# Four MLP blocks of 384 tokens beside the decode, a last block of 576, and two visits fewer in each round of the decode

## The chip, the cores and the metric

One core of a Trainium2 chip runs the whole step as one program. The metric is the device time of one execution in microseconds; for the kernel before three executions are known.

## The reference

One layer of a hybrid decoder computes 2048 prompt tokens and 8 sequences of 8 new tokens each, against a paged cache of 8192 past tokens a sequence. In short:

```python
h = rmsnorm(x, norm1_g)
b, c, u, q, k, v = split(h @ w_in)                       # 1024 -> 3*512 + 3*512
y_conv = b * conv3(c * u)
o = rmsnorm(diff_attn(q, k, v), subln_g) * 0.8           # 4 heads, two maps each, ALiBi
x = x + concat(y_conv, o) @ w_out                        # 1024 x 1024
h2 = rmsnorm(x, norm2_g)
x = x + square(relu(h2 @ w_up)) @ w_down                 # 1024 -> 4096 -> 1024
y = rmsnorm(x, final_g)
```

For the prompt `diff_attn` goes over the prompt's own keys; for the new tokens (the decode) over the gathered pages of the cache and the new keys. Everything is float32. Dense products are made from two float32r parts of each operand, three matmuls for a product; the decode's products are plain float32.

## The kernel before

Four stages follow one another on the tensor engine (PE). **The input projection** goes over the tokens in three blocks. **The attention** of the prompt is mixed with the convolution's columns and, at its end, with the output projection of the first 384 tokens. **The MLP blocks**: three `Dense` objects of 384 prompt tokens each (three tiles of 128) run one after the other. **The last block** has the 64 new tokens and the other 896 prompt tokens, in two groups of 448 and 512 columns.

Each block streams all of `w_out`, `w_up` and `w_down` again: 8 + 32 + 32 weight tiles of 512 KB, each of which ACT copies to its high part (`wh`, L226) and DVE subtracts to its low part (`wl`, L228). `run` goes over 16 chunks of two weight tiles: `up` (L199 to L201) streams a group's tokens past 128 columns of `w_up`, so the moving width is the group's width; `down` (L1410 to L1412) streams 512 columns of `w_down` past 128 tokens. Before the last chunk's `down` comes the output projection of the next block (`out_proj`, L1299 to L1301), and in the last chunk's `down` its normalised tokens are transposed (`turn`, L1267). `before_last` issues the loads of the next block's mixed input ahead of that.

**The decode** is a generator that the dense code advances. Each dense product calls `between(us)`, which pops a pending closure or else calls `tick(us)`; this adds the product's nominal time to a counter, and once the counter has reached `gap * gs` it runs the generator to its next `yield cost, gap`. Such a piece of decode work between two dense products is called a visit here. Two sequences run beside the input projection, then the generator pauses for the attention; the other six run beside the MLP blocks (`gs` is `GS[0]` in the first, `GS[2]` in the second part). `hold` stops it from the last tile of an output projection to the first products of the next block.

A round of the decode takes a pair of chunks of four pages. DVE transposes the keys (`kt`, L717); PE makes the score maps c = 0 and 1 (`sps`, L902, 16 records a map); for the sequence before, PE transposes the exponentials (`pps`, L937), ACT copies them out (`ptt`, L940), and PE multiplies them with the values of the two chunks e = 0 and 1 (`o_ps`, L949, 32 records a chunk, four heads side by side in 32-column strips of the array). A round has a visit for each map, one for the transposes and one for each value chunk. Behind each value chunk `gather_v` (L707) issues the four indirect DMAs for the chunk after next into the same buffer; there are two such buffers (`vpg`). A sequence has 8 rounds; its values come one sequence behind its scores, so that the first 8 rounds of a part have no values and its last 8 no scores.

When the decode is done, `switch` gives its memory to the last block, whose loads are then issued at `poll` places of the last 384-token block, and what is left in `before_last`, after `drain` has run what is left of the decode.

## Time and profile before

| | us |
|---|---|
| median of three runs | 3242.1 |
| the three runs | 3237.74, 3242.1, 3257.38 |
| span of the profiled execution | 3153.6 |
| median less span | 88.5 |
| MLP block 1 starts | 1141 |
| output projections of blocks 2, 3 and of the last | 1474, 1934, 2341 |
| decode's second part, first and last visit | 1168, 2221 |

The span goes from the first to the last instruction of the profiled execution. No time of that execution other than its span is known; the median of the runs is 88.5 us longer, which is what lies around the span. [...]

### The profile page before, as it was taken

To read this page: it belongs to the slowest core of one execution; us is meant where nothing else is said; L and a number is where in the kernel's file an instruction comes from. 1 tells how busy PE (TensorE), PEld (TensorE's weight loads), DVE (VectorE), ACT (ScalarE), POOL (GpSimd) and SP (SyncE) were. 2 spreads that over 40 slices of the span, in tenths; PEclk is the share of its full clock that TensorE was granted. 3 is DMA by queue.
4 is the path that set the end of the run, shared out by engine and by line. 5 is a ranking of instruction groups with operands and counts; after the bars stand their busy time and mean duration, and the time that the engine had idled before them with its cause. 6 is when DMAs were issued, how large, how long until landed. Compare 5 with 4: busy or idle time off the path is not lost. (4 is left out here: it accounts for less than half of the span.)

```text
span 3153.6 us, 53285 instructions
## 1 busy us (share of the span) xinstructions
PE 3014.2 (96%) x20902; PEld 2532.3 (80%) x20902; DVE 1824.8 (58%) x3751; ACT 1243.3 (39%) x2705; POOL 891.8 (28%) x1266
## 2 busy tenths in 40 slices
PE   7999998999999989999999999999999999999998
PEld 7988887989997788777677777777887788888886
DVE  5376353268888668766676776663653444444444
ACT  3323323357778643333343333343332332222222
POOL 0013355211122121455466564467002010000002
PEclk9999999999999999999999999999999999999999
DMA  4777876754335457899689899677741112111111
GB/s 149 229 232 247 286 255 200 223 140 113 108 99 146 139 176 242 278 320 334 229 288 360 304 347 328 211 274 263 230 145 41 61 54 67 47 54 47 54 47 64
DMA packets 400821, 585.80 MB, mean 186 GB/s; under 512 B 35413, under 2 KB 299605, under 8 KB 384186
## 3 DMA queue, kind: packets, MB, share of 16 engines
q1 hardware_dynamic: 337418, 301.07, 31.1%
q0 software_dynamic: 61984, 277.91, 24.5%
q8 instruction: 165, 2.70, 0.3%
q10 hardware_dynamic: 1168, 3.41, 0.3%
q14 instruction: 86, 0.70, 0.1%
HBM read 526.56 MB, written 55.74 MB: 185 GB/s over the span
## 5 line engine op out<-in xcount | busy, mean ns | idle before, releaser
L707 POOL DMA_INDIRECT vpg<-in_cache_v_dram,pt x512 | 537.5, 1050 | 232.3 <-issue 134.4
L226 ACT CAST wh<-wraw 128x1024 fp32r<-128x1024 f32 x336 | 350.0, 1048 | 632.2 <-PE dps L1412 277.1
L228 DVE TENSOR_TENSOR wl<-wraw,wh 128x1024 fp32r<-128x1024 f32 x336 | 410.2, 1221 | 236.4 <-ACT wh L226 227.4
L199 PE MATMUL ups<-h2h,wh 128*128 128x384 f32 (+2 forms) x1264 | 462.6, 366 | 4.9 <-DVE x L1417 2.5
L1417 DVE TENSOR_TENSOR x<-dps,x 128x512 f32<-128x512 f32 (+1 forms) x528 | 355.2, 684 | 177.2 <-PE dps L1412 176.7
L1410 PE MATMUL dps<-wh,uh 128*128 128x512 f32 (+1 forms) x1076 | 438.8, 408 | 13.2 <-ACT wh L226 5.6
L201 PE MATMUL ups<-h2h,wl 128*128 128x384 f32 (+2 forms) x1264 | 448.8, 355 | 0.0
L200 PE MATMUL ups<-h2l,wh 128*128 128x384 f32 (+2 forms) x1264 | 447.9, 354 | 0.0
L1411 PE MATMUL dps<-wl,uh 128*128 128x512 f32 (+1 forms) x1076 | 425.5, 395 | 4.3 <-DVE wl L228 3.3
L1412 PE MATMUL dps<-wh,ul 128*128 128x512 f32 (+1 forms) x1076 | 424.2, 394 | 0.0
L199 PE MATMUL ps<-hh,wh 128*128 128x384 f32 (+1 forms) x1152 | 404.6, 351 | 1.1 <-ACT cc L1526 0.7
L201 PE MATMUL ps<-hh,wl 128*128 128x384 f32 (+1 forms) x1152 | 376.5, 327 | 3.1 <-DVE wl L228 3.1
L200 PE MATMUL ps<-hl,wh 128*128 128x384 f32 (+1 forms) x1152 | 376.0, 326 | 0.1
L1369 DVE TENSOR_TENSOR ul<-r,uh 128x384 fp32r<-128x384 f32 (+2 forms) x158 | 93.6, 592 | 438.5 <-ACT uh L1368 438.3
L717 DVE STREAM_TRANSPOSE kt<-kraw 128x512 f32<-128x512 f32 x512 | 316.9, 678 | 5.4 <-DMA kraw<-in_cache_k_dram,idxk 5.4
L699 POOL DMA_INDIRECT kraw<-in_cache_k_dram,idxk x128 | 129.1, 1009 | 565.6 <-DVE kt L717 522.8
L199 PEld LDWEIGHTS ups<-h2h,wh 128*128 128x128 f32 x1264 | 238.5, 189 | 54.4 <-issue 28.7
L1410 PEld LDWEIGHTS dps<-wh,uh 128*128 128x128 f32 (+1 forms) x1076 | 200.8, 187 | 85.8 <-issue 24.1
L1366 ACT ACTIVATE r<-ups 128x384 f32<-128x384 f32 (+2 forms) x158 | 82.8, 524 | 445.0 <-PE ups L201 445.0
L200 PEld LDWEIGHTS ups<-h2l,wh 128*128 128x128 f32 x1264 | 238.9, 189 | 16.6
L201 PEld LDWEIGHTS ups<-h2h,wl 128*128 128x128 f32 x1264 | 238.5, 189 | 15.3
L284 POOL TENSOR_SCALAR ss<-ss 128x1 f32<-128x1 f32 (+1 forms) x33 | 9.5, 289 | 839.5 <-ACT junk L276 838.7
(275 smaller groups left out, 4985.8 us busy)
## 6 DMA issues: line engine op xcount, KB each, us to landing
wraw<-in_w_up_dram SPq DMA_DIRECT2D x128, 512.0 KB, 5.0
wraw<-in_w_down_dram SPq DMA_DIRECT2D x128, 512.0 KB, 3.3
wraw<-in_w_in_dram SPq DMA_DIRECT2D x72, 512.0 KB, 4.4
wraw<-in_w_out_dram SPq DMA_DIRECT2D x32, 512.0 KB, 4.2
x<-in_x_prompt_dram SPq DMA_DIRECT2D x24, 512.0 KB, 7.0
vpg<-in_cache_v_dram,pt POOLq DMA_INDIRECT x512
qt<-QH SPq DMA_DIRECT2D x64, 128.0 KB, 4.5
qt<-QL SPq DMA_DIRECT2D x64, 128.0 KB, 5.0
```

The costliest lines, as they stand in the source:

```text
L199: nc.tensor.matmul(ps, lhsT=wh, rhs=ah, start=first, stop=False)
L200: nc.tensor.matmul(ps, lhsT=wh, rhs=al, start=False, stop=False)
L201: nc.tensor.matmul(ps, lhsT=wl, rhs=ah, start=False, stop=last)
L226: nc.scalar.copy(wh, t)
L228: eng.tensor_sub(wl, t, wh.bitcast(F32))
L699: nc.gpsimd.indirect_dma_start(out=t.rearrange("p a b -> p (a b)"), out_offset=None, in_=ck, in_offset=bass.IndirectOffsetOnAxis(ap=idxk[: ...
L707: nc.gpsimd.indirect_dma_start(out=t[:, g, :], out_offset=None, in_=cv, in_offset=bass.IndirectOffsetOnAxis(ap=idxv[:, 4 * it + g:4 * it + ...
L717: nc.vector.transpose(t[:, e, 16 * j:16 * j + 16].rearrange("p a b -> p (a b)"), kraw[2 * r + e][:, 16 * j:16 * j + 16].rearrange("p a b - ...
L1410: nc.tensor.matmul(ps, lhsT=uh, rhs=wh[:, half], start=(i == 0), stop=False)
L1411: nc.tensor.matmul(ps, lhsT=uh, rhs=wl[:, half], start=False, stop=False)
L1412: nc.tensor.matmul(ps, lhsT=ul, rhs=wh[:, half], start=False, stop=(i == len(ms) - 1))
L1417: nc.vector.tensor_add(xx, ps, xx)
```

## The change

The first three of four changes are in the order of the work; the last is a set of constants.

- `NDS = 4`: four `Dense` blocks of 384 tokens (1536 prompt tokens) run beside the decode; the last block has the new tokens and 512 prompt tokens, in groups of 320 and 256 columns. The weight stream has one more pass.
- The two score maps of a round are one visit (`yield 2.1`), and the two value chunks are one visit (`yield 2.4`); both chunks' gathers are issued behind the merged visit.
- The gap that stood between the maps moves behind the transposes, the one between the chunks to the end of the merged visit.
- `GS` goes from (0.7, 0.7, 0.7) to (0.75, 0.7, 1.15).

With GP2 = (2, 1, 2, 3, 2, 2, 3, 3) the gaps of a full round beside the MLP still add up to 12, now in four visits or pauses where there were six. Lines that only lose comments are left out here.

```diff
-GS = (0.7, 0.7, 0.7)
+GS = (0.75, 0.7, 1.15)
+NDS = 4
...
                     for c in range(2):
                         for db in range(2):
                             for h in range(H):
...
-                        yield 1.05, gp()[0] if c else gp()[1]
+                    yield 2.1, gp()[0]
...
-                    yield 0.4, gp()[3]
+                    yield 0.4, gp()[3] + gp()[1]
                     for e in range(2):
                         it = NCH * pb + 2 * i + e
                         v = vpg.pop(it)
...
-                        if it + 2 < b1 * NCH:
-                            gather_v(it + 2)
+                    for e in range(2):
+                        if NCH * pb + 2 * i + e + 2 < b1 * NCH:
+                            gather_v(NCH * pb + 2 * i + e + 2)
                         more(MO[3 + e])
-                        yield 1.2, gp()[4 + e]
+                    yield 2.4, gp()[4] + gp()[5]
...
-        W = Weights(wpA, out_weights() + mlp_weights(out_weights()) * 3 + mlp_weights([]), 2, 4, SHR)
-        ds = [Dense([ptiles(384 * i, 384 * i + 384)], ac1, xslots(i), EN1 and nc.gpsimd) for i in range(3)]
+        W = Weights(wpA, out_weights() + mlp_weights(out_weights()) * NDS + mlp_weights([]), 2, 4, SHR)
+        ds = [Dense([ptiles(384 * i, 384 * i + 384)], ac1, xslots(i), EN1 and nc.gpsimd) for i in range(NDS)]
...
-        slots = xslots(3) + [(sm, f"x1_{ti}") for ti in range(3, 8)]
-        d = Dense([[(xs, ys, 0, NS)] + ptiles(1152, 1536), ptiles(1536, 2048)], sm, slots, ENG and nc.gpsimd)
+        slots = xslots(NDS) + [(sm, f"x1_{ti}") for ti in range(3, 5)]
+        t0 = 384 * NDS
+        d = Dense([[(xs, ys, 0, NS)] + ptiles(t0, t0 + 256), ptiles(t0 + 256, T)], sm, slots, ENG and nc.gpsimd)
...
-        elif box and box["todo"] and cur[0] == 2:
+        elif box and box["todo"] and cur[0] == NDS - 1:
...
-        if cur[0] < 2:
+        if cur[0] < NDS - 1:
...
-        if i < 2:
+        if i < NDS - 1:
             rest.append(lambda: load_gain("2", nc.gpsimd))
-        if i == 0:
-            rest += [lambda ti=ti: ds[2].load_x(ti, nc.gpsimd) for ti in range(3)]
+        if i < NDS - 2:
+            rest += [lambda i=i, ti=ti: ds[i + 2].load_x(ti, nc.gpsimd) for ti in range(3)]
```

## Rows read from the trace of the kernel before

**Rows 1.** The page of the profiled execution, its parts 1 and 2: busy time of the tensor engine (PE) with its share of the span, and the busy tenths of GpSimd (POOL, which issues the gathers of the decode) in 40 slices of 78.8 us.

```profile
PE 3014.2 (96%) x20902; PEld 2532.3 (80%) x20902; DVE 1824.8 (58%) x3751; ACT 1243.3 (39%) x2705; POOL 891.8 (28%) x1266
...
POOL 0013355211122121455466564467002010000002
```

**Rows 2.** Busy time by stage: the stretch, its length, then busy us and number of instructions of PE, PEld (weight loads), DVE, ACT and POOL, the granted clock of PE, the DMA share and GB/s. In order: input projection with the decode's first two sequences; MLP block 1; from the output projection of block 2 to that of block 3; block 3 while the decode still runs; the rest of block 3; the last block behind its output projection.

```profile
112.00:612.00 500.00, 478.08 (x4136) 428.64 (x4135) 238.56 (x483) 162.43 (x348) 171.82 (x186) 0.99 0.74 239
1141.00:1474.00 333.00, 324.88 (x2528) 258.22 (x2529) 247.83 (x441) 124.69 (x225) 127.84 (x122) 0.99 0.84 288
1474.00:1934.00 460.00, 437.29 (x3940) 333.58 (x3939) 313.79 (x579) 167.07 (x333) 269.02 (x289) 0.99 0.87 309
1934.00:2221.00 287.00, 266.20 (x2305) 208.18 (x2303) 162.55 (x281) 108.43 (x216) 159.62 (x185) 0.96 0.74 253
2221.00:2341.00 120.00, 116.56 (x580) 105.36 (x581) 72.28 (x100) 48.73 (x71) 0.00 (x0) 0.99 0.68 219
2437.00:3154.00 717.00, 700.34 (x3140) 577.57 (x3138) 308.92 (x436) 193.72 (x290) 45.76 (x106) 0.99 0.18 56
```

**Rows 3.** The timeline of PE around one visit to the score maps (L902) between products of the output projection: start, length, instruction, count.

```profile
1515.87 0.39 PE L1301 MATMUL ps<-wh,mxl 128*128 128x512 f32 x1
1516.19 1.07 PE L902 MATMUL sps<-kt,qbd 128*32 128x256 f32 x16
1517.19 0.50 PE L1299 MATMUL ps<-wh,mxh 128*128 128x512 f32 x1
1517.53 0.40 PE L1300 MATMUL ps<-wl,mxh 128*128 128x512 f32 x1
```

**Rows 4.** The same around a visit to one chunk of cached values (L949, 32 records) and, in the second half, around the visit to the new tokens' values at the end of a sequence (L975, 8 records of the same kind).

```profile
1502.78 0.39 PE L1301 MATMUL ps<-wh,mxl 128*128 128x512 f32 x1
1503.10 1.07 PE L949 MATMUL o_ps<-vpg,ptt 128*16 128x128 f32 x32
1504.10 0.50 PE L1299 MATMUL ps<-wh,mxh 128*128 128x512 f32 x1
1504.43 0.40 PE L1300 MATMUL ps<-wl,mxh 128*128 128x512 f32 x1
...
1631.11 0.40 PE L1412 MATMUL dps<-wh,ul 128*128 128x512 f32 x1
1631.43 0.41 PE L975 MATMUL o_ps<-vn_s,pttn 64*16 64x128 f32 x8
1631.77 0.50 PE L1410 MATMUL dps<-wh,uh 128*128 128x512 f32 x1
1632.11 0.40 PE L1411 MATMUL dps<-wl,uh 128*128 128x512 f32 x1
```

**Rows 5.** The timeline of PE for narrow products: in the input projection the change from 384 to 320 columns, each product with a weight tile of its own; in the attention six score products of 256 columns, and what starts behind them.

```profile
200.78 0.34 PE L201 MATMUL ps<-hh,wl 128*128 128x384 f32 x1
200.96 0.30 PE L199 MATMUL ps<-hh,wh 128*128 128x320 f32 x1
201.10 0.31 PE L200 MATMUL ps<-hl,wh 128*128 128x320 f32 x1
201.25 0.31 PE L201 MATMUL ps<-hh,wl 128*128 128x320 f32 x1
...
750.81 0.98 PE L1832 MATMUL asc<-kst,qt 128*128 128x256 f32 x6
751.63 0.38 PE L1908 MATMUL aT<-ident,S 128*128 128x128 f32 x2
```

**Rows 6.** Waits of PE at the change from block 1 to block 2, 1474 to 1541 us: who waited for whom, us in total, times, longest.

```profile
PE ps L1299 <- ACT wh L226: 3.2, 1, 3.2
PE ps L1300 <- DVE wl L228: 2.7, 3, 1.2
PE tps L1267 <- DVE x L1417: 1.6, 1, 1.6
PE tps L1267 <- DVE h2l L1270: 1.6, 1, 1.6
```

**Rows 7.** The same at the change from block 2 to block 3, 1934 to 2002 us, the waits that rows 6 don't have.

```profile
PE o_ps L949 <- ACT ptt L940: 4.1, 1, 4.1
...
PE dps L1410 <- ACT wh L226: 1.0, 1, 1.0
PE dps L1411 <- DVE ss L286: 0.8, 1, 0.8
```

**Rows 8.** The two longest waits of PE while the decode runs beside the MLP, 1141 to 2241 us.

```profile
PE o_ps L949 <- DMA vpg<-in_cache_v_dram,pt: 14.4, 18, 1.9
PE o_ps L949 <- ACT ptt L940: 10.0, 4, 5.0
```

**Rows 9.** The same for the decode's first two sequences, 112 to 612 us.

```profile
PE o_ps L949 <- DMA vpg<-in_cache_v_dram,pt: 6.2, 7, 2.3
PE o_ps L949 <- ACT ptt L940: 3.3, 2, 1.7
```

**Rows 10.** The timeline around one late page: two of the eight value gathers of a pair of chunks on POOL (the second of them, and the last of the second chunk), then the last piece of the first chunk's value products on PE, which begins when its page lands (in brackets the idle time before it).

```profile
1674.71 0.95 POOL L707 DMA_INDIRECT vpg<-in_cache_v_dram,pt  x1 [0.30 <-issue]
...
1683.28 0.94 POOL L707 DMA_INDIRECT vpg<-in_cache_v_dram,pt  x1 [0.30 <-issue]
...
1686.77 0.41 PE L949 MATMUL o_ps<-vpg,ptt 128*16 128x128 f32 x8 [0.86 <-DMA vpg<-in_cache_v_dram,pt]
```

More of the change, by code (lines that the diff above doesn't have):

```diff
@@ L2080, in switch @@
                        for gi in range(2) for g in range(2) for x in "hl"]
-        box["todo"] += [lambda ti=ti: d.load_x(ti) for ti in list(range(3, 8)) + list(range(3))]
+        box["todo"] += [lambda ti=ti: d.load_x(ti) for ti in list(range(3, 5)) + list(range(3))]
     def poll():
@@ L2103, in tile_hymba_step @@
         cur[0] = i
-        d.run([(sb1, "uh", "ul", 4, 384)], poll, before_last, lambda: ds[cur[0] + 1] if cur[0] < 2 else box["d"], None)
+        d.run([(sb1, "uh", "ul", 4, 384)], poll, before_last, lambda: ds[cur[0] + 1] if cur[0] < NDS - 1 else box["d"], None)
         rest += [lambda: load_gain("f", nc.gpsimd)] + FN * [lambda: None]
```

## The prediction

> **What bounds the kernel now.** I read the page first, then busy time by stage, then the timeline of the tensor engine around the places that the change touches, and last its waits. PE is busy for 96% of the span [rows 1], so only what PE does, or waits for, can move the end. Its lengths overlap; what a product costs is the distance from one start to the next, and the sums below are made of such distances. By stage [rows 2] the kernel is uneven: from 1141 to 2221 us, where six of the eight sequences run beside the MLP, the DMA share is 0.74 to 0.87, and in the 717 us of the last block it is 0.18. GpSimd's digits tell the same [rows 1]: gathers stand in slices 4 to 8 and 17 to 29, and the last ten slices have almost none. The change spreads the decode over more dense work, at the price of one more pass over the weights, and makes three visits of five.
>
> **Fewer visits.** Without a visit a product of 512 columns takes 0.23 us: 717 us over 3140 in the last block [rows 2]; 1517.53 less 1517.19 is 0.34 because the first one behind a visit is late [rows 3]. From the last product before the score visit (1515.87) to the second one behind it (1517.53) are 1.66 us; less two distances of 0.23 that is 1.20 us for the visit. For the values [rows 4] it is 1504.43 less 1502.78, 1.65 less 0.46, or 1.19 us for 32 records; and the small visit, 8 records of the same kind, takes 1632.11 less 1631.11, 1.00 less 0.46, or 0.54. So 24 records more cost 0.65 us, 8 cost 0.22, and 0.32 us of a visit belong to no record: they are paid at the change from full-array products to column strips and back. The score visit shows the same pieces [rows 3]: 0.09 us before it, about 0.13 behind its last group, 0.11 at the product after. Two merges in each of 64 rounds (8 sequences of 8) save 128 times 0.32, **41 us**: 31 beside the MLP, 10 in the input projection. Bounds: only the two pieces that are read directly (0.09 and 0.11), 26 us; if the small visit's records cost nothing of their own, all of its 0.54, 69 us. I take 41, the value that both kinds of visit give. It lies on the path, since PE has no slack.
>
> **The same products in other widths.** `down` and the output projection always stream 512 columns for each tile, and there are 17 tiles before and after: no change. `up` streams the group's width, and the groups 448 and 512 become 384, 320 and 256, each 768 products. The distance is 0.18 to 0.175 at 384 columns and 0.147 at 320 [rows 5], 0.00044 us a column and some 0.006 to 0.012 that no column explains. Three groups instead of two pay that piece 768 times more: **+4 to +9, taken as +5 us**. For 256 columns six starts to the next product take 0.82 us, at most 0.137 each [rows 5], against 0.12 by the slope; the row as it stands would make it +13.
>
> The extra pass over the weights is 72 tiles of 512 KB, with their casts on ACT and subtractions on DVE. Block for block this is work of the kind that the stage already holds, with DVE busy for 314 and ACT for 167 of 460 us [rows 2]. From 1141 to 2341 the four stretches give 337 MB in 1200 us, 281 GB/s [rows 2]. With 38 MB and one block of about 290 us more it becomes 375 MB in some 1480 us, 253 GB/s: the stage where PE waits for pages and weights gets lighter by a tenth, and I cost the pass itself at nothing. Without that cover a tile late by 1 us each time would cost 72 us.
>
> **One more change of blocks.** At a change PE waits for the output weights, which queue on SP behind the next block's mixed input, and for the norms and transposes. The four waits of the first change add up to 9.1 us [rows 6]; the second has 1.8 us beside the 4.1 of the decode's own [rows 7], and the two waits of 1.6 for the transposes again, 5.0 in all. The granted clock falls to its lower level around such waits (0.96 as the mean from 1934 to 2221 us [rows 2], so 23 us at half speed, 11 lost); I count 2 to 4 us of that for a change. The third change that the decode now sees costs 7 to 13 us: **+10**. The change to the last block keeps its form; with 3 and 2 tiles in its groups instead of 4 and 4, fewer products cover the norms: **+3**, 0 to 6.
>
> **The transposed exponentials.** PE waits 10.0 us beside the MLP and 3.3 before for ACT's copy `ptt` [rows 8, 9], in six places, the longest 5.0 and 4.1. Between transposes and values stood 3 gaps times 0.7, 2.1 us of dense work; now it is 4 times 1.15, 4.6, and 5 times 0.75, 3.75 in the first part. Each wait shrinks by 1.6 to 2.5 us and the short ones go: **-9 us**, and with the two long ones some of the lower clock, **-3**. ACT is in order: a copy that stands behind two weight casts can be late all the same, so the bounds are 0 and -16.
>
> **The pages.** PE waits 14.4 and 6.2 us for them [rows 8, 9]. The reason is seen at one late page: gathers follow each other on POOL at 1.43 us (8.57 for six), eight take 11 us, and a piece came 3.5 us behind the last issue of its pair while its own issue lay further back [rows 10]. Behind a merged visit all eight gathers are issued together, from about 1.5 us on; the last page is there after 1.5 + 11 + 4, about 16.5 us. A full round took 12 x 0.7 = 8.4 us of gaps, some 2 for rounding each up to the next product, and 5.2 of visits, about 16; it will take 13.8 + 1.5 + 4.6, about 20. That leaves 3.5 us, as much as the second chunk had before. In the first part, with 13 x 0.75, a round has only 16, and its rounds without scores about 11, but pending closures stretch most of these. What is queued behind a waiting visit on PE is dense work, so a late page is paid in full. One more block's gains, results and tokens also pass POOL's queue ahead of gathers. I take **0**, with -10 (a lighter DMA) and +15 (the first part's short rounds, that queue) as bounds.
>
> **Does the decode end in time?** In dense microseconds its second part needs 37 to begin, 8 rounds without values of about 17.6, 40 full ones of 15.3, 8 without scores of 12.7, and 12 at each of six sequence ends: about 970, and before, by the same reckoning, 650. The trace needed about 720 (1080 us from 1141 to 2221, less 48 rounds of 5.2, some 80 of waits and lower clock, and two stretches of 14 under `hold`), so I raise 970 by a tenth to 1070. A block of 384 has 720 products of 512 columns at 0.23 and 768 of 384 at 0.174, 299 us; the first has 258 left behind the attention. Four offer 3 x 299 + 258, less three stretches of 14: 1113. It ends some 40 to 80 us before the last block's output projection. `drain` finds nothing, but the last block's loads have less time than the 120 us of before [rows 2].
>
> **The sum.** -41 + 5 + 10 + 3 - 9 - 3 + 0 = -35 us. The profiled span is 3153.6 us, so the new one is about 3119; its own time outside the span isn't given, and I carry over the 88.5 us by which the median of the three runs, 3242.1, exceeds it: **3207 us**, 1.1% less. The three runs lie 20 us apart, so a change within 1% (32 us) can hardly be told from none.
>
> **Rivals.** *What is saved at the visits is mostly given back, chance 0.33.* The extra change costs 13 us, 256 columns cost 0.137 us a product (+13), the copies stay late: -41 + 13 + 13 + 3 - 3 = -15, 3227 us. For it: every piece except the merges is small and uncertain. Against: the copy's gap doubles.
>
> *The lower rate clears the waits, 0.17.* Most of the 34 us of waits for pages and copies [rows 8, 9] go, with half of the lower clock (-5), and the rest as forecast: -41 + 5 + 10 + 3 - 30 - 5 = -58, 3184. For it: 281 to 253 GB/s, longer rounds; against: the wait for a page is set by GpSimd's issue, not by bytes [rows 10].
>
> *Merged value visits wait for the second chunk, 0.05: slower.* Place: the second half of each merged visit. It decides once the last of eight gathers lands later than a round, 20 us beside the MLP; 3.5 are left [rows 10], so another 4 us on POOL (a key gather of 1 us that waits for DVE, norms) use it up. If each of the 56 rounds beside the MLP waited 2 us more, +112, less the other gains of 35: +77, 3319. Against: such waits came in 18 of 96 visits and were 0.8 us on average [rows 8]; a wait also gives POOL time to catch up.
>
> *Narrow products are bound by their weight loads, 0.03: slower.* In the last block a load has a length of 0.184 us (577.57 over 3138) [rows 2]. If it hid behind nothing, 256 and 320 columns would take at least 0.184: 768 x (0.064 + 0.037), +78, 3285 us. Against it stands 0.147 at 320 columns, each with its own weights [rows 5]. [...]
>
> *The change doesn't do what it says, 0.02*: the decode isn't done when block 4 ends, and `drain` runs the rest bare, with its chain of copies exposed; 5 rounds at 5 us more, +25 on the forecast, 3232.
>
> **How the numbers follow.** The forecast itself, 3195 to 3218, has 0.40. The range that leaves out 2 in 10 is **3176 to 3241**: it takes in the second rival, the first with its bounds, and the decode's late end, not the two slower ones. Faster by over 1% (below 3209.7) takes 0.23 of the forecast's chance, all of the second rival's 0.17 and 0.10 of the first's that lie at its better bounds: 0.50. Slower by over 1% (above 3274.5) is the two slower rivals, less what a milder form gives: 0.07. The rest is 0.43.
>
> **What the new profile would show.** Right: 64 score visits of 32 records and 64 value visits of 64, each about 2.05 us by starts; three changes of blocks with 5 to 9 us of waits; `ptt` below 5 us in the waits; the DMA share around 0.75 beside the decode; `up` at 256 columns 0.12 to 0.137 us apart; last decode visit 40 to 80 us before the last output projection. Wrong: page waits above 30 us, a change of blocks above 15, or narrow products at 0.18.

## The result, and the profile after

The changed kernel took 3296.1 us (median of four runs), the kernel before 3249.7 in runs beside it: ratio 1.0140, 95% interval 1.0099 to 1.0182. The forecast was 3207 us, 1.1% less; the time is 1.4% more. The profiled execution of after has a span of 3301.5 us and a time of 3303.3: 1.8 us lie around the span, not 88.5 as the table ahead of the prediction has it.

That difference is the first finding, and the rest can't be read without it. The runs of this study came from different chips, and the same kernel before took 3254.7 and 3275.0 us on two of them and 3156.1, 3157.0 and 3154.9 on three others. The trace shown ahead of the prediction (span 3153.6) agrees with the three; the three times shown beside it (3242.1) and the result above agree, by their length, with the two. In what follows a chip of the **first kind** is one where before takes 3240 us or more, one of the **second kind** one where it takes about 3155. Each chip was seen on one occasion only, so that what is called a kind of chip may as well be a state that it was in. A ratio is always to before on the same chip.

From the page of after: busy time of PE, the digits of GpSimd and of PE's granted clock in 40 slices, and the queue that brings instructions.

```profile
PE 3060.2 (93%) x21670; PEld 2638.1 (80%) x21670; DVE 1910.0 (58%) x3861; ACT 1332.0 (40%) x2873; POOL 889.1 (27%) x1274
...
POOL 1022244201221121224454333544334520110001
PEclk9998998999999999999999999999999999999999
...
q8 instruction: 171, 2.80, 0.3%
```

PE's share of the span falls from 96% [rows 1] to 93%, and GpSimd's gathers now reach over four blocks. By stage (length, then busy time and instructions of PE, PEld, DVE, ACT and POOL, granted clock, DMA share, GB/s): the input projection behind the first 112 us, the four blocks, the last one.

```profile
112.00:706.00 594.00, 535.89 (x4334) 484.26 (x4332) 246.73 (x494) 169.47 (x364) 166.33 (x186) 0.94 0.65 211
1098.00:1511.00 413.00, 389.27 (x2456) 331.51 (x2455) 279.63 (x512) 180.77 (x355) 85.19 (x127) 0.97 0.60 199
1511.00:1957.00 446.00, 406.74 (x3201) 326.19 (x3201) 272.80 (x476) 157.16 (x293) 189.63 (x218) 0.97 0.74 253
1957.00:2397.00 440.00, 403.02 (x3202) 327.77 (x3201) 271.18 (x472) 156.41 (x291) 192.10 (x217) 0.97 0.74 253
2397.00:2786.00 389.00, 360.94 (x2578) 306.89 (x2577) 215.96 (x339) 151.56 (x265) 131.43 (x155) 0.97 0.64 211
2786.00:3301.50 515.50, 497.17 (x2815) 429.20 (x2813) 250.52 (x363) 172.98 (x302) 39.06 (x100) 0.99 0.25 82
```

Against [rows 2] two things changed: the granted clock (0.94 in the input projection, where before had 0.99, and 0.97 in all four blocks) and PE's busy share of the blocks (0.91 to 0.94, where before had 0.93 to 0.98). In the whole trace PE stood at the lower of its two levels (0.50, against 1.00) for 210 us, in before for 88. At the lower one a product of 384 columns takes 0.32 us from start to start (475.22 to 475.54), at the upper one 0.18 (479.34 to 479.52); with half of it counted as lost, the 121 us more are worth 61. The input projection is 62 us longer than in the trace of before (594 against 532, both from 112 us to the first score product of the attention), though no block was added there.

What PE waited for, after: first in the input projection (112 to 706 us), then from the first output projection to the last (1098 to 2786 us); in us, times, longest.

```profile
...
PE sps L903 <- issue: 9.3, 18, 1.0
...
PE o_ps L950 <- DMA vpg<-in_cache_v_dram,pt: 3.3, 3, 1.9
```

```profile
PE dps L1413 <- DVE wl L229: 29.5, 21, 5.1
PE ups L200 <- DVE x L1419: 13.8, 7, 5.1
PE sps L903 <- issue: 13.7, 23, 1.0
PE dps L1412 <- ACT wh L227: 11.0, 5, 4.6
PE ps L1302 <- DVE wl L229: 7.7, 6, 3.0
```

The waits of [rows 8] and [rows 9] have all but gone: pages 3.3 us, copies 3.0 in both stretches together (1.9 of them `ptt`, the rest the copy for the new tokens). Two others stand in their place. Weights that are cast and subtracted too late (all lines of the second view that name `wh` or `wl` give 54.9 us; 12.4 in the trace of before), and "issue" at the score visits, time in which the engine waited for nothing that the trace shows.

By their median the visits are what the sum took them for. The timeline of PE in after, around a score visit, a value visit, and in the last block's `up` at 256 columns:

```profile
1289.98 0.40 PE L1414 MATMUL dps<-wh,ul 128*128 128x512 f32 x1
1290.31 1.93 PE L903 MATMUL sps<-kt,qbd 128*32 128x256 f32 x32
1292.17 0.50 PE L1412 MATMUL dps<-wh,uh 128*128 128x512 f32 x1
1292.51 0.40 PE L1413 MATMUL dps<-wl,uh 128*128 128x512 f32 x1
...
1706.42 0.39 PE L1414 MATMUL dps<-wh,ul 128*128 128x512 f32 x1
1706.74 1.94 PE L950 MATMUL o_ps<-vpg,ptt 128*16 128x128 f32 x64
1708.61 0.50 PE L1412 MATMUL dps<-wh,uh 128*128 128x512 f32 x1
1708.94 0.40 PE L1413 MATMUL dps<-wl,uh 128*128 128x512 f32 x1
...
3015.37 0.28 PE L200 MATMUL ups<-h2h,wh 128*128 128x256 f32 x1
3015.49 0.28 PE L201 MATMUL ups<-h2l,wh 128*128 128x256 f32 x1
```

By starts less two distances of 0.23, as in [rows 3] and [rows 4]: 2.53 less 0.46 is 2.07 us for the scores, 2.52 less 0.46 is 2.06 for the values. The median over all 64 of each kind, from the last product ahead to the first behind, is 2.18 and 2.19; the means are 3.10 and 2.41. The distance at 256 columns is 0.119 us, the median of 753.

A score visit in the input projection shows where the mean of the scores comes from:

```profile
466.57 0.33 PE L202 MATMUL ps<-hh,wl 128*128 128x384 f32 x1
466.84 1.06 PE L903 MATMUL sps<-kt,qbd 128*32 128x256 f32 x14
468.14 0.64 PE L903 MATMUL sps<-kt,qbd 128*32 128x256 f32 x5 [0.24 <-issue]
469.57 0.63 PE L903 MATMUL sps<-kt,qbd 128*32 128x256 f32 x4 [0.79 <-issue]
470.99 1.10 PE L903 MATMUL sps<-kt,qbd 128*32 128x256 f32 x5 [0.80 <-issue]
472.45 1.03 PE L903 MATMUL sps<-kt,qbd 128*32 128x256 f32 x3 [0.36 <-issue]
473.87 0.61 PE L903 MATMUL sps<-kt,qbd 128*32 128x256 f32 x1 [0.39 <-issue]
474.42 0.69 PE L200 MATMUL ps<-hh,wh 128*128 128x384 f32 x1
```

The first 14 records start at once; the others come up to five at a time, the groups 1.43 us apart, and the visit takes 7.9 us in place of 2.2. None of these instructions has a wait. Call such places **gaps**: 0.6 to 1.3 us from one start to the next before an instruction without a wait, counted from 112 us on, less 0.23 each. After has 56 of them, 35.6 us in all.

### The profile page after: what moved, and what is told of

The parts are those of the page before. It is cut to its first block, busy times and chain, and to the rows that moved or that the text cites. A ratio compares the mean times of both kernels' runs of the same rounds, so it can differ in the third digit from the quotient of the medians.

```text
span 3301.5 us, 55431 instructions
## 1 busy us (share of the span) xinstructions
PE 3060.2 (93%) x21670; PEld 2638.1 (80%) x21670; DVE 1910.0 (58%) x3861; ACT 1332.0 (40%) x2873; POOL 889.1 (27%) x1274
## 4 chain that ended last, share of the span: by engine, by line
PE 58%; issue 14%; POOL 9%; DVE 8%; DMA 5%; ACT 4%; another core or an unknown queue 2%; SPq 0%; ACTq 0%; POOLq 0%; DVEq 0%
POOL vpg L708 6%; PE ups L200 5%; PE ups L202 5%; PE dps L1413 5%; PE dps L1414 5%; PE dps L1412 5%; PE ups L201 5%; PE ps L200 4%; PE ps L202 4%; PE ps L201 4%; PE asc L1834 3%; PE O L1921 3%; PE sps L903 2%; DVE kt L718 2%; PE o_ps L950 2%
## 5 line engine op out<-in xcount | busy, mean ns | idle before, releaser
L227 ACT CAST wh<-wraw 128x1024 fp32r<-128x1024 f32 x408 | 425.6, 1048 | 681.2 <-PE dps L1414 168.5
L229 DVE TENSOR_TENSOR wl<-wraw,wh 128x1024 fp32r<-128x1024 f32 x408 | 500.4, 1227 | 318.7 <-ACT wh L227 273.5
L708 POOL DMA_INDIRECT vpg<-in_cache_v_dram,pt x512 | 528.9, 1033 | 357.8 <-PE o_ps L950 215.2
L200 PE MATMUL ups<-h2h,wh 128*128 128x384 f32 (+2 forms) x1520 | 501.0, 330 | 17.6 <-DVE x L1419 13.8
L202 PE MATMUL ups<-h2h,wl 128*128 128x384 f32 (+2 forms) x1520 | 494.2, 325 | 5.7 <-DVE wl L229 4.1
L201 PE MATMUL ups<-h2l,wh 128*128 128x384 f32 (+2 forms) x1520 | 492.0, 324 | 0.7 <-issue 0.7
L200 PEld LDWEIGHTS ups<-h2h,wh 128*128 128x128 f32 x1520 | 288.1, 190 | 39.3 <-issue 27.0
L202 PEld LDWEIGHTS ups<-h2h,wl 128*128 128x128 f32 x1520 | 288.0, 189 | 9.1 <-DVE wl L229 6.1
L201 PEld LDWEIGHTS ups<-h2l,wh 128*128 128x128 f32 x1520 | 288.5, 190 | 4.2 <-issue 1.7
L1413 PEld LDWEIGHTS dps<-wl,uh 128*128 128x128 f32 (+1 forms) x1076 | 203.6, 189 | 84.8 <-DVE wl L229 44.2
```

Source lines behind the costliest of these rows:

```text
L200: nc.tensor.matmul(ps, lhsT=wh, rhs=ah, start=first, stop=False)
L201: nc.tensor.matmul(ps, lhsT=wh, rhs=al, start=False, stop=False)
L202: nc.tensor.matmul(ps, lhsT=wl, rhs=ah, start=False, stop=last)
L227: nc.scalar.copy(wh, t)
L229: eng.tensor_sub(wl, t, wh.bitcast(F32))
L708: nc.gpsimd.indirect_dma_start(out=t[:, g, :], out_offset=None, in_=cv, in_offset=bass.IndirectOffsetOnAxis(ap=idxv[:, 4 * it + g:4 * it + ...
```

## The experiments

Four theories. *Occasion*: the trace of before is of an execution that does not stand for its times. *Supply*: at certain places of the program PE gets its instructions late, and a visit of many records that falls there is drawn out. *Pages*: merged value visits wait for the second chunk (the third rival of the prediction). *Pace*: the wider gap of 1.15 beside the MLP has a price of its own. Two of these are called otherwise in the first expectations: instruction theory stands for supply, and pass theory there says that the extra pass over the weights costs the time.

### Both kernels and each half of the change, on a chip of the first kind (before 3254.7)

**Before, unchanged.** 

> The kernel before, unchanged, so that its profile comes from the same chip as the others'. Occasion theory: the profiled execution that the forecast used (span 3153.6 us) was some 85 us faster than its timed runs, and what lies around a span is 2 us, as in the profile of the changed kernel (3303.31 against 3301.5); then this profile has a span of 3235 to 3262 us and its PE waits for 'issue' inside the score visits and for late weight parts (over 30 us together), as the changed kernel's. Change theory: the profile is like the first (span about 3155, no such waits), and those waits are the change's own.

Ratio 1.0007 (0.9976 to 1.0037), span 3244.8 us: the base is 91 us above the trace of before, as the occasion theory had it, and 1.8 lie around the span. There are 46 gaps of 28.0 us; the trace of before has none. Two lines of its waits that the earlier trace doesn't have:

```profile
PE sps L902 <- issue: 13.2, 21, 1.0
...
PE o_ps L949 <- issue: 9.8, 17, 1.6
```

**The merges alone** (three blocks, gaps of 0.7).

```
-                        yield 1.05, gp()[0] if c else gp()[1]
+                    yield 2.1, gp()[0]
...
-                    yield 0.4, gp()[3]
+                    yield 0.4, gp()[3] + gp()[1]
...
-                        yield 1.2, gp()[4 + e]
+                    yield 2.4, gp()[4] + gp()[5]
```

> The merged visits alone, with three blocks of 384 and the old pace. Instruction theory (a visit of 32 score matmuls in a row outruns the supply of PE's instructions): the 41 us of saved switches are taken back by 'issue' waits inside the score visits, 64 visits at 0.9 us, 58 us, so +10 to +25 us on the kernel before. Pass theory (the extra pass and change of blocks cost the time): -25 to -45 us.

3327.7 us, ratio 1.0243 (1.0198 to 1.0289). That is some 75 us more than before, far over the 10 to 25 of the instruction theory, and against the pass theory. 65 gaps of 38.0 us, 41 waits for pages of 40.3 us, 249 us at the lower clock against 129. The input projection behind 112 us takes 593 us, 549 in before on this chip.

**The blocks alone** (four of 384 and one of 576, gap of 1.15, five visits; against before).

```
-GS = (0.7, 0.7, 0.7)
+GS = (0.7, 0.7, 1.15)
+NDS = 4
```

> Four blocks of 384 and the slower pace beside the MLP (GS 0.7, 0.7, 1.15), with the old five visits a round. Pass theory: +40 to +80 us on the kernel before, and the changed kernel is faster than this one by 25 to 45. Instruction theory: +10 to +25 us (the one more change of blocks), with few 'issue' waits.

3225.1 us, ratio 0.9926 (0.9903 to 0.9948): faster than both kernels on this chip, where both theories had expected it slower. 9 gaps of 4.9 us, 134 us at the lower clock, but 47.8 us of waits for weights beside the MLP.

**After, again.** 

> The changed kernel again, beside the three others on one chip: +35 to +60 us on the kernel before by all theories. If the occasion theory holds, the sum of its waits exceeds that of the profile of the kernel before taken here by no more than 60 us, not by 150.

3284.6 us, ratio 1.0125 (1.0075 to 1.0174). So here blocks and pace give 24 us and the merges take 65 (1.0125 less 0.9926 of 3254.7); by the medians it is 30 and 59. With the merges the gap of the first part went from 0.7 to 0.75, so the 65 are of both. 40 of them stand in the input projection, where two of the eight sequences run: 586 us behind 112 us, 546 with the blocks alone. 45 gaps of 29.4 us, where the same program without merges has 4.9. The gaps are not scattered: of the 64 score visits, numbers 10, 14 and 16 took 9.7, 7.6 and 7.8 us in the trace of after and 8.7, 7.8 and 8.2 here, and none of the first nine met a gap in either. Of the 17 visits in each trace that took over 1 us more than the median, 13 are the same, one of them late only through a wait for its keys. Most belong to places of the program.

### Halves and pace, on a chip of the second kind (before 3156.1)

**Score maps merged, values not** (blocks and gap as in the run with the blocks alone). 

> The four blocks and gaps of 0.7, 0.7, 1.15 as in the run with the blocks alone (3225.1 us), and of the merges only that of the two score maps; the value chunks stay two visits. The supply theory: at certain places of the program PE goes on with four records every 1.43 us although no instruction waits for anything (23.6 us of such gaps inside score visits after the change, 2.2 with the blocks alone), a visit of 32 score records that falls on such a place is drawn out, and the lower clock follows. It expects 3255 to 3285 us, 15 us or more of such gaps in score visits, and over 170 us at the lower clock. The page theory: the merges lose through the value visits, which wait for the second chunk. It expects 3205 to 3225 here.

3197.6 us, ratio 1.0126 (1.0088 to 1.0164), and no gap at all in the trace, in this run or in any other of this kind of chip. As a ratio the supply theory's range was 1.000 to 1.009 and the page theory's 0.985 to 0.991. It is above both, and what PE waits for beside the MLP are weights, 54.5 us.

**Values merged, score maps not.** 

> The other half: blocks and gaps as in the run with the blocks alone, value chunks in one visit, the two score maps in two. The supply theory expects 3205 to 3230 us (64 changes of mode at 0.32 us saved, some pages later) and fewer than 8 us of gaps in score visits. The page theory expects 3255 or more, with over 30 us of waits for pages.

3197.3 us, ratio 1.0148 (1.0105 to 1.0190). No gap; pages 15.9 us, half of what the page theory wanted, and weights 65.1 beside the MLP. What both runs share with each other, and not with before, are the four blocks and the pace.

**Four blocks at the old pace**, five visits (the line of the pace, against after).

```
-GS = (0.75, 0.7, 1.15)
+GS = (0.7, 0.7, 0.7)
```

> Four blocks of 384 and a last one of 576, five visits as before the change, and all gaps 0.7 as before. It tells the extra block from the pace. If the gain of the blocks alone (3225.1 against 3254) comes from the wider gap of 1.15 beside the MLP, this is at or over the kernel before: 3254 plus 5 to 15 for the third change of blocks and the narrower groups, 3255 to 3270, and the decode ends before the fourth block is half done. If the gain comes from the blocks (a shorter last block, more dense work), it is 3220 to 3235.

3168.5 us, ratio 1.0045 (1.0024 to 1.0066): the extra block costs 14 us (8 to 21), as the first case of the expectation had it. PE's waits:

```profile
PE o_ps L950 <- DMA vpg<-in_cache_v_dram,pt: 21.6, 26, 2.4
...
PE o_ps L950 <- ACT ptt L941: 13.6, 10, 4.5
...
PE dps L1411 <- ACT wh L227: 5.4, 3, 2.5
...
PE dps L1412 <- DVE wl L229: 4.4, 8, 1.0
```

Pages and copies as in the kernel before, and hardly any wait for weights, although the extra pass over them is there.

**Half of the score products left out.** 

> The changed kernel with half of the score products left out (one of the two halves of the inner dimension), so that the merged visit has 16 records, as many as a split one had; all visits, gaps, transfers and copies stay. By the medians of the visits (2.18 us with 32 records, 1.30 with 16) the missing work is worth 64 times 0.88, 56 us. The supply theory expects that the gaps inside score visits go too (below 5 us, from 23.5) and a good part of the extra lower clock (45 us at half speed against the blocks alone): 3284.6 less 56, 19 and some 15 is about 3195, at most 3210. If the loss has another place (value visits, the gathers issued together, the longer rounds), only the 56 go: 3228, with the lower clock at 175 us or more.

3147.3 us, ratio 0.9974 (0.9957 to 0.9992). On a chip without gaps it can't tell the supply theory. Against after on this kind of chip (next) it gave 24 us for 56 of missing work: PE waits more for weights (66.5 us beside the MLP, 56.7 in after) and stands longer at the lower clock (164 against 151).

### After, and the pace without and with merges, on a second chip of that kind (before 3157.0)

**After, once more.** 

> The changed kernel once more, because the first four runs and the next four came from different chips: the kernel before took 3254.7 us on the one and 3156.1 on the other, where no trace shows a gap of 0.6 to 1.3 us without a wait. If this chip is of the second kind: the pace theory (the gap of 1.15 makes weight subtractions late on DVE, 50 to 65 us of waits in the MLP in all four runs that have it, 13.6 where the gap is 0.7) expects a ratio to before of 1.010 to 1.020, with 50 us or more of waits for weights beside the MLP; the supply theory alone expects 0.985 to 1.0, since without those gaps the forecast should come true. If it is of the first kind, 1.0125 again.

3173.2 us, ratio 1.0051 (1.0035 to 1.0067). No gap. The visit shown above, the sixteenth to the scores, takes 2.13 us here:

```profile
427.43 0.33 PE L202 MATMUL ps<-hh,wl 128*128 128x384 f32 x1
427.69 1.93 PE L903 MATMUL sps<-kt,qbd 128*32 128x256 f32 x32
429.56 0.45 PE L200 MATMUL ps<-hh,wh 128*128 128x384 f32 x1
```

and the input projection behind 112 us takes 528.7, where it took 594 and 586 on chips of the first kind. Still it is 16 us slower than before, with 56.7 us of waits for weights: above the supply theory's range, and at half of the least that the pace theory gave.

**The blocks alone, once more.** 

> Blocks and gaps of 0.7, 0.7, 1.15 without merges, again, on the chip of this call. On a chip of the first kind 0.993 as there. On one of the second kind the pace theory expects about what the two half merges gave, 1.010 to 1.020, or 1.015 to 1.030 if the merges are worth their 20 us each; the supply theory, by which the merges alone lose, expects 0.985 to 1.005.

3206.9 us, ratio 1.0162 (1.0132 to 1.0193), in the pace theory's range. Its waits:

```profile
PE dps L1412 <- DVE wl L229: 31.5, 22, 4.1
...
PE ps L1301 <- DVE wl L229: 11.4, 8, 4.4
...
PE o_ps L950 <- DMA vpg<-in_cache_v_dram,pt: 4.8, 4, 2.2
```

All lines on `wh` and `wl` beside the MLP give 56.9 us, 13.6 at a gap of 0.7. The only edit between the two runs is the pace, and it costs 37 us (1.0162 less 1.0045, of 3156; the two ran on two chips of this kind). With the merges added, and 0.75 in the first part (the run before this one), 35 us come back.

Where such a weight is late can be followed back in the two traces. In 35.7 of the 56.9 us the subtraction began right behind other work of DVE, so it stood in DVE's order; at 0.7 in 2.6 of 13.6. In 11.9 us it was the transfer of the raw weights that came last, at 0.7 in 5.9. A median of 6.6 us of unbroken work lay ahead of those subtractions on DVE, and half of it, 3.2 us on average, were the decode's key transposes. DVE and PE around one such place:

```profile
2161.02 3.08 DVE L718 STREAM_TRANSPOSE kt<-kraw 128x512 f32<-128x512 f32 x5
...
2164.60 1.20 DVE L229 TENSOR_TENSOR wl<-wraw,wh 128x1024 fp32r<-128x1024 f32 x1
2165.73 1.89 DVE L718 STREAM_TRANSPOSE kt<-kraw 128x512 f32<-128x512 f32 x3
...
2167.97 1.21 DVE L229 TENSOR_TENSOR wl<-wraw,wh 128x1024 fp32r<-128x1024 f32 x1
...
2169.24 0.50 PE L1412 MATMUL dps<-wl,uh 128*128 128x512 f32 x1 [2.42 <-DVE wl L229]
```

PE waits for the last of these subtractions, whose cast had ended at 2164.62. Five of the round's eight transposes held up the subtraction ahead of it, the other three its own.

**Merges and four blocks, all gaps 0.7.** 

> The changed kernel with all gaps at 0.7. It tells the pace from the merges: compared with the run of four blocks, five visits and 0.7 (ratio 1.0045 on the second kind of chip) only the merges differ. Pace theory on such a chip: waits for weights under 25 us, the merges save up to 41 us and lose some of it to pages (40 us of waits in the run with the merges alone): ratio 0.990 to 1.010. If the merges lose by themselves, whatever the pace, 1.015 or more. On the first kind of chip the supply theory expects 1.010 to 1.025.

3247.1 us, ratio 1.0290 (1.0260 to 1.0319): at this pace the same merges lose 77 us against the run with five visits; between these two only the merges differ.

```profile
PE o_ps L950 <- DMA vpg<-in_cache_v_dram,pt: 60.5, 87, 3.7
```

87 waits for pages in place of 26, and 216 us at the lower clock against 110. The third rival is real; it decides at 0.7 and not at 1.15 (60.5 us of waits for pages here, 6.0 in after on this chip). Some 26 of the 77 us stand in the input projection, 552.6 us behind 112 us against 527.1; with 0.75 there, as in after, it takes 528.7.

**Before with the score maps merged**, one gap a round dropped.

```
-                        yield 1.05, gp()[0] if c else gp()[1]
+                    yield 2.1, gp()[0]
```

> The kernel before with the two score maps in one visit and nothing else changed; the gap between the maps goes, so a round is 1.4 to 2.1 us of dense work shorter. By the visits' medians 64 changes of mode at 0.32 us go, 20 us: ratio 0.994 if nothing is given back. If the merged visit loses by itself on any chip (lower clock behind it, later pages in the shorter round): 1.003 or more. On a chip with the gaps without a wait: 1.005 to 1.015.

3209.0 us, ratio 1.0172 (1.0147 to 1.0198): 52.3 us of waits for pages and 26.7 for `ptt`, on a chip without gaps. Nothing touched the value visits; the round became shorter, and the pages late.

### Why weights are late, on a third chip of that kind (before 3154.9)

**Splits issued earlier.**

```
-WD = (.2, .7)
+WD = (0., .4)
```

> The changed kernel with the splits of the next weights issued earlier in a down product: at its first and third of six steps, not the second and fifth. It tests why weights are late at the gap of 1.15 (57 us of waits beside the MLP): if it is the place of the split in the program, with the cast and the subtraction behind other work of ACT and DVE that is issued first, these waits fall below 30 us and the time by 20 to 45 us. If the raw weights come late from memory (ACT waits for them), the place changes nothing: within 8 us of the changed kernel, and the same 50 to 60 us.

3198.8 us, ratio 1.0139 (1.0103 to 1.0175). Neither expectation holds. The waits for weights fall to 39.3 us beside the MLP, but those for DVE's other results (sums `x`, transposed tokens, norms and the rest) rise from 35.4 in after on this kind to 62.0. Together they are 101.3 us, and 92.1 in after: here the order on DVE changed who was late, not whether someone was.

**A gap of 0.95.** 

> The changed kernel with 0.95 in place of 1.15 beside the MLP. With the merges a gap of 0.7 makes the value visits wait for pages (60.5 us in all) and one of 1.15 does not (6.0), but has 57 us of waits for weights against 30. If the two trade smoothly, 0.95 has 10 to 25 us of pages and 35 to 50 of weights, and the time is within 0.6% of that at 1.15; a clear gain of 0.8% or more would mean that the pace alone was set wrong.

3167.2 us, ratio 1.0038 (1.0018 to 1.0059), like 1.15. Weights 30.7 us, pages 16.0: the two trade, with less left for weights than the 35 to 50 expected.

**The two half merges again.** 

> Four blocks, gap 1.15, score maps merged, values in two visits, once more: ratio 1.0126 on the second kind of chip. There it tells little new. If this call falls on a chip of the first kind (before near 3250), the supply theory expects it 30 us or more behind the blocks alone, ratio 1.002 to 1.014, with 12 us or more of gaps without a wait inside score visits; the page theory 0.987 to 0.995.

> Four blocks, gap 1.15, value chunks merged, score maps in two visits, once more: ratio 1.0148 on the second kind of chip. On one of the first kind the supply theory expects 0.985 to 0.997 (a gain of up to 20 us over the blocks alone), with under 8 us of gaps without a wait inside score visits; if value visits lose there too, 1.0 or more.

Ratios 1.0158 (1.0128 to 1.0189) and 1.0121 (1.0098 to 1.0144), again on a chip without gaps. Over both pairs the score merge is worth some 6 us and the value merge some 9 against the blocks alone, less than the 35 of both together. Each of these differences is uncertain by about 10, and the 35 hold the gap of 0.75 in the first part, which the halves don't have: their input projections take 530 to 539 us, after's 528.7.

### The score merge with its gap kept, on a second chip of the first kind (before 3275.0)

**The gap moved ahead of the values.**

```
-                        yield 1.05, gp()[0] if c else gp()[1]
+                    yield 2.1, gp()[0]
...
-                    yield 0.4, gp()[3]
+                    yield 0.4, gp()[3] + gp()[1]
```

> The kernel before with the score maps in one visit and the gap between them not dropped (that cost 1.0172) but moved to the place between the transposes and the values, as the change does. Nothing else differs: three blocks, gaps of 0.7, value chunks in two visits. On a chip where PE has no gaps without a wait: 64 changes of mode at 0.32 us go, 20 us, and the copies ptt get the wider gap (9 to 13 us of waits before), while a page of the second chunk has 0.3 us less: ratio 0.988 to 0.997, with 15 to 25 us of waits for pages. If pages still decide (over 40 us), 1.005 or more. On a chip with such gaps the supply theory expects 1.0 to 1.015.

3317.6 us, ratio 1.0131 (1.0109 to 1.0152), in the supply theory's range. 69 gaps of 41.2 us, and only 9.0 us of waits for pages, in 13 places.

```profile
PE o_ps L949 <- ACT ptt L940: 26.4, 13, 5.3
PE o_ps L949 <- issue: 22.9, 33, 4.1
...
PE sps L902 <- issue: 12.6, 23, 1.0
```

**The gap right behind the scores.** 

> The same with the dropped gap put right behind the score visit. The copies ptt keep their 2.1 us and wait as before (10 to 14 us), the pages have as long as in the other run: 0.992 to 1.0, 5 to 10 us behind the other where the wider gap at the copies is what pays; the same where it is only the length of the round.

3291.3 us, ratio 1.0053 (1.0030 to 1.0076): 26 us better than the other, against the expectation. `ptt` waits 31.5 us and pages 23.9, both more; what is less are the gaps, 45 of 25.2 us, and the lower clock, 178 us against 208.

No version beat both kernels everywhere. On a chip of the first kind the blocks alone do (0.9926); on one of the second kind before is ahead of every version that computes all of it.

## Why the prediction was wrong

**The base: near in its level, wrong in what stood behind it.** "I carry over the 88.5 us by which the median of the three runs, 3242.1, exceeds it" joined a trace and times that belong to two kinds of chip. The time around the span is 1.8 us. As the sum so went up to the median of the timed runs, three of which are among the result's four of before, the level is off by 8 us only; with the measured base of either kind the forecast of 35 us less would read 3121 against 3173, or 3215 against 3296. What the joining hid weighs more: the prices were read in a trace without a gap, and applied where there are gaps.

**The merges: the step that failed where the result was taken.** -41 us; with the first part's 0.75 it is +65 on the first kind, and this alone turns the forecast's gain into a loss there. The price of 0.32 us a visit comes from visits that nothing drew out; the median still bears it out (2.18 us), the mean of the merged score visits does not (3.10). Of the loss the traces show 24.5 us more gaps (4.9 to 29.4), 45 us more at the lower clock (worth 22) and more waits behind them. On the second kind the price held at the pace of the change, -35 (0.75 in the first part included); at 0.7 it is +77 there, through pages. A visit of 64 records in 1.94 us has one in 0.03 us, where dense work has one in 0.23; but a split visit, 32 in 1.07 [rows 4], has them as close; what the split visits had was dense products in between. That the length of the burst meets the gaps is one reading, and it is not shown: before the change, without any merge, there were as many gaps (46 of 28.0 us) as in the last run above with the score maps merged (45 of 25.2). What places them in a program is open, and so is what the value merge by itself does on the first kind.

**The widths, the third change of blocks, the last block: right.** +5, +10 and +3 make 18; the run with four blocks at 0.7 gives +14 (8 to 21). 256 columns take 0.119 us, by the slope and not by the row of [rows 5]. Each of these products has a weight tile of its own, whose load has a length of 0.188 us. The loads, too, start 0.12 us apart, and each with the product ahead of its own (the one for the product at 3015.49 at 3015.37), so they overlap each other and the products. The three changes of after show 9.6, 9.1 and 13.5 us of waits, over the 5 to 9 that were given as a sign of being right and under the 15 of being wrong.

**The pass over the weights and the pace: the step that failed on the second kind.** "I cost the pass itself at nothing", since the stage's transfers got lighter. They did: 199 to 253 GB/s after, 230 on average, where 253 was forecast. The pass alone does cost nothing (13.6 us of waits for weights with four blocks at 0.7). It is the wider gap, which the sum had at -9 and -3, that brings 43 us of waits for weights, 37 us in all. 33 of the 43 are subtractions that stand behind other work of DVE, the decode's key transposes above all; 6 are transfers. The weights wait on the first kind too (47.8 us, 15.3 in before). The bound "a tile late by 1 us each time would cost 72 us" was written and not used. Why the wider spacing puts the transposes there stays open; one reading, not shown, is that steps which used to end in a wait for a page or a copy let ACT and DVE catch up. Moving the split or narrowing the gap only trades.

**`ptt`, pages, the end of the decode: right, and worth little.** 3.0 us of copies, 3.3 of pages, the last decode product at 2699 us, 87 ahead of the last output projection (40 to 80 given). That a copy can be late behind a cast is in the trace of before: the transposes of one round began by 1595.6 us, but ACT stood 6.28 us for raw weights, their cast began at 1602.26, the copies `ptt` behind it at 1603.21, and PE stood 5.04 us for them. Most of what was listed as a sign came true or nearly so, and the time was 89 us off. A sign that shows a cost gone says nothing of what takes its place.

**The lower clock: wrong in sign.** -3 us; it grew from 88 to 151 us in the span on the second kind (worth +31) and from 129 to 179 on one chip of the first. In the trace of after 37 of the 41 falls to the lower level come shortly behind an idle stretch of PE of over 1 us, in before 21 of 22.

So on the second kind: blocks +14, pace +37, merges -35, sum +16. On the first: blocks and pace -24 together, merges +65, sum +41; the result's own runs gave +46. None of the five rivals had either loss in its place.

Two things stay open: what makes the gaps, and why blocks and pace gain 24 us on the first kind and cost 51 on the second, 75 apart. 23 us of the 75 are gaps that are not there (28.0 to 4.9). The time at the lower clock grows by 5 us on the first kind (129 to 134) and by 36 on the second (88 to 124), a difference worth 15; the waits for weights grow by 32 (15.3 to 47.8) and by 44 (12.4 to 56.9), a difference of 12. The rest is not accounted for.

## What to carry over

Hold the span of the trace against the timed runs before anything is added to it: where they are further apart than the time around a span, they may not be of the same chip, and a sum made on one does not hold on the other. An edit that clears a wait is worth what the next late engine leaves of it (on the second kind the waits for pages and `ptt` fell from 33.9 us in before to 6.0 in after, and those for weights beside the MLP rose from 12.4 to 56.7); put the number of that engine (here DVE's subtraction, behind the key transposes) into the sum, with the bound and not with zero. A longer burst on one engine can be cheaper by its median and dearer by its mean (the merged score visit 2.18 us by the median and 3.10 by the mean, two split ones in the trace of before 2.54 and 2.66), so look at both.

## What was not expected of the hardware

The same kernel took 3155 to 3157 us on three chips and 3255 and 3275 on two, and what the traces show to differ is the supply of PE: 46 gaps of 28.0 us in before on the one kind, none on the other; DVE is late in the same way. In the trace of before on a chip of the first kind it has 33 idle stretches, 83 us in all, that no wait ended in the trace; one line of its waits:

```profile
DVE wl L228 <- issue: 23.0, 14, 7.7
```

The other traces of this kind have 22 to 44 of them (60 to 139 us), the blocks alone too (39), where PE has hardly a gap. On the second kind no trace has one, but for 0.4 us in the trace ahead of the prediction. If these are late instructions too, which the trace does not show, then it is not PE alone that gets them late, nor bursts alone that meet it. No duration of an instruction that was compared differs: casts take 1048 ns by the median, subtractions 1218 to 1219, gathers 947, in the trace ahead of the prediction, which agrees with the second kind, as in the result's trace of after, on the first.

In the gaps of the visit shown PE gets three to five records every 1.43 us. Queue 8, which the page calls that of instructions, has 171 transfers in after, 2.80 MB or 16 KB each, and about 1.0 us long. But no such transfer lies in that visit (466.84 to 474.42): the nearest begin at 459.1 and 475.0. The queues that moved anything from 467 to 475 us, with packets, MB and share of 16 engines:

```profile
q0 software_dynamic: 592, 1.91, 63.2%
q1 hardware_dynamic: 283, 1.03, 32.5%
```

So the gaps are not the wait for such a transfer as far as the trace can show. The DMA engines are busy for 96% of that stretch, but busy engines alone don't make a gap: in after on the second kind 42 of the score visits without one have a DMA share over 0.9. What the gaps are is not settled.
